# A planner told other TensorE times, and the end of the last norm spread over three engines

## The chip, the cores and the metric

The kernel runs on one core of one Trainium2 chip. The metric is device microseconds of one execution; a difference of about 0.2% is the least that a measurement of this kernel can tell from none. TensorE (PE; its weight loads are PEld) multiplies, VectorE (DVE) and ScalarE (ACT) do elementwise work, GpSimd (POOL) does small odd jobs, and SyncE (SP) issues every DMA.

## The reference, cut to what matters

Two decoder layers on 256 tokens of width 1024, all in float32. Layer 0 mixes tokens by a gated unit in chunks of 128, layer 1 by attention with 16 heads (256 tokens are one block, so it is plain causal attention with a relative bias). After each mixer comes a gated MLP of width 2816 with a causal convolution of width 3. Each of the four sub-layers ends in

```
x = layer_norm(alpha * x + f(x), g, b)      # over the 1024 columns of each token
y = (x - mean) * rsqrt(var + eps) * g + b
```

The last of these norms is the output. The kernel computes it for a tile of 128 tokens in two steps: first `(x - mean) * g`, then `that * rstd + b`.

## The kernel before, in words

Tokens lie in two tiles of 128 (`t` = 0, 1). A float32 product is made of three products of split operands (`hi*hi`, `hi*lo`, `lo*hi`, type float32r); for a weight chunk of 1 MB, ScalarE writes `whi` (a rounded copy) and VectorE `wlo` (the rest). One step (`rows_step`, line 553) for one row block `k`, one tile `t` and 512 output columns is a group of three matmuls.

Nothing is issued as it is written down. Every operation is recorded in a `Plan` (line 74) with an engine, an estimated time and its dependencies. `Plan.emit` (line 122) then runs a list scheduler over the records and issues everything in the order that this yields. TensorE's bulk groups keep their recorded order; short groups marked `fill` (transposes, attention, spatial mixing) go in as soon as the plan says that they are ready. On the other engines the operation that can start first is taken, and among those that can start together the one with the earliest due time; when these are equal, the one that became a candidate first. Between engines the plan adds `LATE` (line 82: pe 200, act 140, dve 130, pool 200 ns, and 150 more when TensorE is the one that waits, line 213), and 130 ns between dependent operations of one engine. For a DMA, SP is taken to be held for 475 ns. These engine queues are in order on the chip: an instruction that waits holds all that stand behind it on its engine, and all DMAs stand in SP's one queue.

The estimates: a float32r matmul of n columns `max(107, n/2.4) + 2.5` ns (line 322), a float32 one 218 ns up to 128 columns and `n/0.6 + 5` above, a transpose 110 ns; VectorE's `stt` (line 346) 130 + 1.04 n with a per-token scalar, 70 + 1.04 n without; `ts` (line 350) 187 + 0.52 n; an activation (line 335) 93 + 0.833 n, and 93 more for each per-token operand. `plan.later(ns, fn)` records `fn` once TensorE's recorded time has advanced by `ns`; `plan.tick(AHEAD)` records what falls due in the next 12 us.

`project_out` (line 583) is the last product of each sub-layer, with its norm. It runs all but the last 6 row blocks for both tiles, then finishes tile 0: its first 512 columns over the 6 blocks, then its other 512. Then tile 1: 512 columns, and two pieces of 256 columns in banks of their own. `stats` (line 487) adds each finished piece to the residual, runs bn_stats on it, aggregates, adds eps, and has GpSimd raise the variance to -0.5 (line 500) for `rstd`. For the inner norms `ln_back` (line 518) normalizes on VectorE (`ts`, line 351), turns the tile with transposes (fills, line 332) and splits it for the next product. For the last norm `scaled` (line 504) does the two steps on VectorE, in two halves of 512 columns and in four pieces of 256, each stored by a DMA of 128 KB (line 355). The end of tile 1's `scaled` is the end of the kernel.

Of the kernel before, what the change touches and what calls it, by code (L numbers as in the profile page):

```python
# [12 lines left out]
F32R = mybir.dt.float32r  # L13
AF = mybir.ActivationFunctionType
ALU = mybir.AluOpType
# [3 lines left out]
P = 128  # L19
D = 1024  # L20
# [5 lines left out]
NT = S // P  # L26
# [9 lines left out]
HALF = 512  # L36
# [11 lines left out]
AHEAD = 12000  # L48
# [167 lines left out]
def flat(ap):  # L216
    n = 1
    for d in ap.shape[1:]:
        n *= d
    return n  # L220
# [3 lines left out]
def trunk_kernel(ctx: ExitStack, tc: tile.TileContext, a: dict, out: bass.AP):  # L224
    nc = tc.nc
    plan = Plan()
# [58 lines left out]
    def bank(long=False):  # L285
        free = [i for i in ALONE if not bank_of[i][2]]
        return taken(min(free, key=lambda i: bank_of[i][0]), long) if free else half(long)
# [29 lines left out]
    def mms(seq, r, w, fill=False):  # L317

        ns = 0.0
        for o, l, x, _, _ in seq:  # L320
            n = flat(x)
            ns += max(107.0, n / 2.4) + 2.5 if l.dtype == F32R else (218.0 if n <= P else n / 0.6 + 5)

        def emit():
            for o, l, x, start, stop in seq:
                nc.tensor.matmul(o, l, x, start=start, stop=stop)  # L326
        plan.op("pe", ns, emit, r, w, fill)

    def transposes(seq, r, w):
        def emit():  # L330
            for o, x in seq:
                nc.tensor.transpose(o, x, ident.ap)  # L332
        plan.op("pe", 110.0 * len(seq), emit, list(r) + [ident], w, True)

    def act(o, x, func, r, w, bias=None, scale=None, accum=None, psum=False, table=None):
        kw = {k: v for k, v in (("bias", bias), ("scale", scale), ("accum_out", accum)) if v is not None}
        ns = (51 if psum else 93) + 0.833 * flat(x) + 93 * (sum(not isinstance(v, float) for v in kw.values()))
        plan.op("act", ns, lambda: nc.scalar.activation(o, x, func, **kw), r, w, table=table)  # L338

    def dve(ns, emit, r, w):  # L340
        plan.op("dve", ns, emit, r, w)
# [4 lines left out]
    def stt(o, x, s, y, op0, op1, r, w):  # L346
        dve((70 if isinstance(s, float) else 130) + 1.04 * flat(x),
            lambda: nc.vector.scalar_tensor_tensor(o, x, s, y, op0=op0, op1=op1), r, w)  # L348
# [4 lines left out]
    def load(o, src, w, r=(), nbytes=None, rank=None):  # L353
        nbytes = nbytes or flat(o) * P * 4
        plan.op("sp", nbytes / 360.0, lambda: nc.sync.dma_start(o, src), r, w, nbytes=nbytes, rank=rank)  # L355
# [50 lines left out]
    def sub(name, c, s):  # L406
        return chunks[where[name, c]][s]

    def spent(name, c):
        i = where[name, c] + CHUNKS  # L410
        if i < len(stream):
            prep(i)


    def const(name, cols):
        return Buf(sb.tile([P, cols], F32, name=name))

    ident, nhalf = const("ident", P), const("nhalf", 1)
# [4 lines left out]
    def xt_new():  # L423
        return xth.new(), xtl.new()
# [24 lines left out]
    def ln_rows(i):  # L449
        b = rowring.new()  # L450
        src = a["lnrow"]
        load(b.ap, bass.AP(tensor=src.tensor, offset=src.offset + i * 2 * D, ap=[[0, P], [1, 2 * D]]), [b])
        return b, b.ap.rearrange("p (a d) -> p a d", a=2)
# [47 lines left out]
                [(st, ["ve"]), nhalf], [(st, ["rstd"])])  # L501
        return st, mv[:, 0:1], rstd

    def scaled(r, x, st, mean, rstd, rows, to=None):

        rb, rv = rows
        for o in range(0, D, HALF):
            sl, parts = slice(o, o + HALF), range(o // S, (o + HALF) // S)
            stt(x[:, sl], x[:, sl], mean, rv[:, 0, sl], ALU.subtract, ALU.mult,
                [(r, parts), (st, ["mv"]), rb], [(r, parts)])  # L510
        for o, n in [(o, S) for o in range(0, D, S)]:
            sl, parts = slice(o, o + n), range(o // S, (o + n) // S)
            stt(x[:, sl], x[:, sl], rstd, rv[:, 1, sl], ALU.mult, ALU.add,
                [(r, parts), (st, ["rstd"]), rb], [(r, parts)])
            if to is not None:
                load(to[:, sl], x[:, sl], (), [(r, parts)])

# [65 lines left out]
    def project_out(name, nk, at, xold, li, rows_i):  # L583

        last = li is None

        rows = None if name == "b_o" else ln_rows(rows_i)


        pieces = [[(o, HALF, bank(True)) for o in (0, HALF)] for _ in range(NT)]  # L590
        cuts = [[(0, HALF), (HALF, HALF)], [(0, HALF), (HALF, S), (HALF + S, S)]]
        ends = []

        def step(t, k, which, first=0, last=nk - 1):
            hi, lo = sub(name, k // 2, k % 2)
            hk, lk, r = at(k, t)
            rows_step(which, hk, lk, r, hi, lo, k == first, k == last)

        start = nk - TAIL
        for k in range(start):  # L600
            for t in range(NT):
                step(t, k, pieces[t][:1])
                step(t, k, pieces[t][1:], last=nk - 1 if t == 0 else start - 1)
            if k % 2:
                spent(name, k // 2)
        res = (None, None) if last else xt_new()
        for t in range(NT):
            r, x = xold[t], xold[t].ap

            def add(o, n, b, by=ALPHA):  # L610
                parts = range(o // S, (o + n) // S)
                stt(x[:, o:o + n], x[:, o:o + n], by, b.ap[:, :n], ALU.mult, ALU.add, [(r, parts), b], [(r, parts)])
                done_with(b)

            mine = list(pieces[t])
            if t == NT - 1:
                add(*mine.pop())
                ends = [(o, n, half()) for o, n in cuts[t][1:]]
                mine += ends
            for p in mine:  # L620
                for k in range(start, nk):
                    if t == 0 and k == nk - 2:
                        plan.tick(AHEAD)
                    step(t, k, [p], first=start if p in ends else 0)
            if t == NT - 1:
                for k in range(start, nk, 2):
                    spent(name, k // 2)

            rows = rows or ln_rows(rows_i)
            st, mean, rstd = stats(r, x, cuts[t], lambda j, o, n: add(*mine[j], 1.0 if mine[j] in ends else ALPHA))  # L630
            if last:
                scaled(r, x, st, mean, rstd, rows, out[t * P:(t + 1) * P, :])
            else:
                ln_back(r, st, mean, rstd, rows, t, li, *res, T0_WAITS if t == 0 else T1_WAITS)
        return res
# [244 lines left out]

    at = gmlp()
    h, l = project_out("a_out", KT, at, xtok, 0, 1)
    at = conv_up(0, h, l)
    scr = build_bias(10 * S)
    h, l = project_out("f_dn0", FT, at, xtok, 1, 2)
    at = moba(h, l, scr)
    h, l = project_out("b_o", KT, at, xtok, 2, 3)
# [82 lines left out]
```

## Time and profile before

| | us |
|---|---|
| median of 3 runs | 572.33 (572.28 to 572.41) |
| profiled execution | 571.2 |
| its span, first to last instruction | 569.5 |

| engine | busy us | share of the span |
|---|---|---|
| PE | 556.1 | 98% |
| DVE | 464.3 | 82% |
| ACT | 359.2 | 63% |
| POOL | 11.5 | 2% |

The chain of work that ended last is 95% PE. A busy share is an average over stages: a gain counts only where that engine's work is what ends last. Busy PE means that matmuls are in flight, and the trace models their ends, so the distance between starts is what shows its pace.

### The profile page before, as it was taken

What the parts mean: (1) busy time and instruction counts of PE and PEld (TensorE: products, weight loads), DVE (VectorE), ACT (ScalarE), POOL (GpSimd) and SP (SyncE); (2) the same over time, 40 slices, a digit from 0 to 9 for tenths busy, and PEclk for the clock granted to TensorE, in tenths of its full rate; (3) what the DMA queues carried; (4) which work ended last, traced back from release to release, by engine and by line L of the source; (5) the groups of instructions that cost most, each with busy time, mean ns of one, the idle gap of its engine ahead of it and who ended that gap; (6) DMA issues with size and microseconds to landing.
All of it is one profiled execution on the core that took longest, in us unless ns stands there. A gap on an engine that the chain in (4) does not pass through costs nothing.

```text
span 569.5 us, 8289 instructions
## 1 busy us (share of the span) xinstructions
PE 556.1 (98%) x3098; PEld 474.9 (83%) x3098; DVE 464.3 (82%) x873; ACT 359.2 (63%) x652; POOL 11.5 (2%) x17
## 2 busy tenths in 40 slices
PE   6999999999999999999999999999999999999994
PEld 4799888888888878888888877788888888888884
DVE  5598989999999997467958988579989999996526
ACT  5555558776777686335578877377777767775300
POOL 0020010000000000001000000010000000000001
PEclk9999999999999999999999999999999999999998
DMA  7897435547554577742665653506455556566302
GB/s 266 330 361 283 181 146 182 189 153 279 171 211 155 216 229 266 270 165 74 222 221 185 194 210 115 222 2 221 156 218 219 201 174 218 195 242 229 147 1 74
DMA packets 20132, 110.92 MB, mean 195 GB/s; under 512 B 2251, under 2 KB 6268, under 8 KB 7676
## 3 DMA queue, kind: packets, MB, share of 16 engines
q1 hardware_dynamic: 20092, 110.39, 54.2%
q8 instruction: 24, 0.39, 0.3%
q14 instruction: 16, 0.13, 0.1%
HBM read 109.31 MB, written 1.07 MB: 194 GB/s over the span
## 4 chain that ended last, share of the span: by engine, by line
PE 95%; DMA 2%; DVE 1%; SPq 0%; ACT 0%; issue 0%; DVEq 0%
PE twos L326 52%; PE bank L326 41%; DMA raw<-in_a_v 2%; PE bank L332 1%; PE twos L332 1%; DVE wlo L344 0%; DVE x L348 0%; SPq L355 0%; ACT whi L338 0%; DVE stat L494 0%; DVEq L966 0%; DVE stat L497 0%; DVE stat L499 0%; DVE xt L344 0%
## 5 line engine op out<-in xcount | busy, mean ns | idle before, releaser
L344 DVE TENSOR_TENSOR wlo<-raw,whi 128x1024 fp32r<-128x1024 f32 (+1 forms) x212 | 228.2, 1099 | 33.7 <-ACT whi L338 32.8
L338 ACT ACTIVATE whi<-raw 128x1024 fp32r<-128x1024 f32 (+1 forms) x212 | 194.8, 954 | 55.1 <-DMA raw<-in_f_dn 21.3
L326 PE MATMUL twos<-xt,whi 128*128 128x512 f32 x640 | 222.2, 394 | 0.0
L326 PE MATMUL twos<-xt,wlo 128*128 128x256 f32 x640 | 177.3, 277 | 0.0
L326 PEld LDWEIGHTS twos<-xt,whi 128*128 128x128 f32 x640 | 120.0, 188 | 27.8
L326 PE MATMUL bank<-whi,rr 128*128 128x512 f32 x432 | 135.5, 391 | 0.0
L326 PEld LDWEIGHTS twos<-xt,wlo 128*128 128x128 f32 x640 | 120.1, 188 | 0.1
L326 PEld LDWEIGHTS bank<-whi,rr 128*128 128x128 f32 x432 | 81.1, 188 | 17.9 <-issue 1.0
L326 PE MATMUL bank<-wlo,rr 128*128 128x512 f32 x216 | 84.0, 389 | 0.0
L326 PE MATMUL bank<-xt,whi 128*128 128x256 f32 (+1 forms) x256 | 71.0, 348 | 0.0
L348 DVE SCALAR_TENSOR_TENSOR ff<-ff,convc 128x254 f32<-128x254 f32 (+1 forms) x160 | 69.6, 478 | 0.3
L338 ACT ACTIVATE ff<-twos 128x512 f32<-128x512 f32 (+1 forms) x56 | 30.8, 565 | 47.9 <-PE twos L326 44.8
L326 PE MATMUL bank<-xt,wlo 128*128 128x256 f32 x192 | 54.0, 281 | 0.0
L326 PEld LDWEIGHTS bank<-xt,whi 128*128 128x128 f32 x256 | 44.0, 190 | 6.8 <-issue 1.0
L326 PEld LDWEIGHTS bank<-wlo,rr 128*128 128x128 f32 x216 | 40.6, 188 | 8.0
L338 ACT ACTIVATE ff<-ff,convc 128x256 f32<-128x256 f32 x80 | 45.6, 592 | 1.9 <-DVE ff L344 1.2
L344 DVE TENSOR_TENSOR ff<-twos,ff 128x512 f32<-128x512 f32 (+1 forms) x48 | 30.9, 645 | 15.3 <-ACT ff L338 13.0
L326 PE MATMUL twos<-whi,xt 128*128 128x512 f32 x128 | 42.1, 396 | 0.0
L338 ACT ACTIVATE ff<-bank,lncol 128x128 f32<-128x128 f32 x48 | 18.8, 458 | 29.1 <-PE bank L332 29.1
L326 PEld LDWEIGHTS bank<-xt,wlo 128*128 128x128 f32 x192 | 36.4, 190 | 0.0
L348 DVE SCALAR_TENSOR_TENSOR x<-x,bank 128x512 f32<-128x512 f32 x16 | 11.0, 686 | 25.0 <-PE bank L326 25.0
L326 PEld LDWEIGHTS twos<-whi,xt 128*128 128x128 f32 x128 | 24.1, 188 | 4.8
(71 smaller groups left out, 489.1 us busy)
## 6 DMA issues: line engine op xcount, KB each, us to landing
raw<-in_f_up SPq DMA_DIRECT2D x44, 1024.0 KB, 4.8
raw<-in_f_dn SPq DMA_DIRECT2D x22, 1024.0 KB, 4.9
raw<-in_b_qk SPq DMA_DIRECT2D x8, 1024.0 KB, 4.9
lnrow<-in_lnrow SPq DMA_DIRECT2D x5, 1024.0 KB, 6.7
raw<-in_a_u SPq DMA_DIRECT2D x4, 1024.0 KB, 5.1
raw<-in_a_out SPq DMA_DIRECT2D x4, 1024.0 KB, 5.0
raw<-in_b_v SPq DMA_DIRECT2D x4, 1024.0 KB, 4.9
raw<-in_b_o SPq DMA_DIRECT2D x4, 1024.0 KB, 5.0
```

The source lines that it names most:

```text
L326: nc.tensor.matmul(o, l, x, start=start, stop=stop)
L332: nc.tensor.transpose(o, x, ident.ap)
L338: plan.op("act", ns, lambda: nc.scalar.activation(o, x, func, **kw), r, w, table=table)
L344: dve(70 + 1.04 * flat(x), lambda: nc.vector.tensor_tensor(o, x, y, op=op), r, w)
L348: lambda: nc.vector.scalar_tensor_tensor(o, x, s, y, op0=op0, op1=op1), r, w)
```

## The change

Three edits. First, the planner's estimates for TensorE: a float32r matmul becomes `n/2.4 + 13.4` ns, a float32 one `n/0.6 - 25`, a group whose stationary operand is under 128 in a dimension takes `0.68 * ns + 200`, and a group of transposes `60 + 93 * len`. No instruction changes by this, only the order in which the plan issues. Second, in `project_out` tile 0 finishes in another order: the last 6 row blocks run without the very last one for both halves, and then the last block for both. Third, in the very last norm (tile 1): the first step takes the upper 512 columns ahead of the lower, and the second step of columns 768 to 1023 goes to ScalarE (`* rstd`) and then GpSimd (`+ b`), with 600 ns as GpSimd's estimate; the other three pieces stay on VectorE.

```diff
@@ mms
-            ns += max(107.0, n / 2.4) + 2.5 if l.dtype == F32R else (218.0 if n <= P else n / 0.6 + 5)
+            ns += n / 2.4 + 13.4 if l.dtype == F32R else n / 0.6 - 25.0
+        if min(seq[0][1].shape) < P:
+            ns = 0.68 * ns + 200.0
@@ transposes
-        plan.op("pe", 110.0 * len(seq), emit, list(r) + [ident], w, True)
+        plan.op("pe", 60.0 + 93.0 * len(seq), emit, list(r) + [ident], w, True)
@@ scaled
-    def scaled(r, x, st, mean, rstd, rows, to=None):
+    def scaled(r, x, st, mean, rstd, rows, to=None, shared=False):
-        for o in range(0, D, HALF):
+        for o in (HALF, 0) if shared else (0, HALF):
...
-            stt(x[:, sl], x[:, sl], rstd, rv[:, 1, sl], ALU.mult, ALU.add,
-                [(r, parts), (st, ["rstd"]), rb], [(r, parts)])
+            if shared and o + n == D:
+                act(x[:, sl], x[:, sl], AF.Copy, [(r, parts), (st, ["rstd"])], [(r, parts)], scale=rstd)
+                plan.op("pool", 600, lambda sl=sl: nc.gpsimd.tensor_tensor(x[:, sl], x[:, sl], rv[:, 1, sl], op=ALU.add),
+                        [(r, parts), rb], [(r, parts)])
+            else:
+                stt(x[:, sl], x[:, sl], rstd, rv[:, 1, sl], ALU.mult, ALU.add,
+                    [(r, parts), (st, ["rstd"]), rb], [(r, parts)])
@@ project_out
-            for p in mine:
-                for k in range(start, nk):
-                    if t == 0 and k == nk - 2:
-                        plan.tick(AHEAD)
-                    step(t, k, [p], first=start if p in ends else 0)
+            todo = [(p, k) for p in mine for k in range(start, nk)]
+            if t == 0:
+                todo.sort(key=lambda x: x[1] == nk - 1)
+            for p, k in todo:
+                if t == 0 and k == nk - 2:
+                    plan.tick(AHEAD)
+                step(t, k, [p], first=start if p in ends else 0)
...
-                scaled(r, x, st, mean, rstd, rows, out[t * P:(t + 1) * P, :])
+                scaled(r, x, st, mean, rstd, rows, out[t * P:(t + 1) * P, :], t == NT - 1)
```

## Rows read from the trace of the kernel before

**Rows 1.** Busy time by stretch: us, each engine's busy us (instructions), PEclk, DMA share, GB/s.
```profile
0.00:20.40 20.40, 14.64 (x49) 10.99 (x50) 9.72 (x21) 10.28 (x17) 0.70 (x6) 1.00 0.83 295
20.40:561.90 541.50, 541.50 (x3049) 463.92 (x3049) 450.49 (x843) 348.87 (x635) 9.88 (x10) 1.00 0.54 193
561.90:569.50 7.60, 0.00 (x0) 0.00 (x0) 4.14 (x10) 0.00 (x0) 0.92 (x1) 0.63 0.21 69
```

**Rows 2.** Waits of PE: for whom, us in total, times, longest us.
```profile
PE bank L326 <- DVE xt L361: 4.9, 1, 4.9
PE bank L326 <- DVE wlo L344: 0.8, 1, 0.8
```

**Rows 3.** The chain that ended last, its head: start us, us, what.
```profile
10.08 0.69 DVE wlo L344
...
10.79 7.21 DMA raw<-in_a_v
...
19.12 1.24 DVE wlo L344
...
20.40 19.62 PE bank L326 x119
```

**Rows 4.** Timeline of PE: start us, us, engine, line, operation, out<-in, shape, count.
```profile
75.51 0.27 PE L332 MATMUL bank<-ident,x 128*128 128x128 f32 x1
...
530.00 0.62 PE L326 MATMUL bank<-whi,rr 128*128 128x512 f32 x2
...
530.68 0.62 PE L326 MATMUL bank<-whi,rr 128*128 128x512 f32 x2
```

**Rows 5.** Timeline of SP's queue at the end.
```profile
565.02 0.33 SPq L355 DMA_DIRECT2D out<-x  x1
...
565.42 0.41 SPq L355 DMA_DIRECT2D out<-x  x1
...
565.93 0.39 SPq L355 DMA_DIRECT2D out<-x  x1
...
566.42 0.40 SPq L355 DMA_DIRECT2D out<-x  x1
```

**Rows 6.** Timeline of DVE at the end (a count merges instructions).
```profile
563.20 0.74 DVE L348 SCALAR_TENSOR_TENSOR x<-x,stat,lnrow 128x512 f32<-128x512 f32 x1
...
563.86 1.14 DVE L348 SCALAR_TENSOR_TENSOR x<-x,stat,lnrow 128x512 f32<-128x512 f32 x2
...
564.52 0.87 DVE L348 SCALAR_TENSOR_TENSOR x<-x,stat,lnrow 128x256 f32<-128x256 f32 x2
...
565.31 0.87 DVE L348 SCALAR_TENSOR_TENSOR x<-x,stat,lnrow 128x256 f32<-128x256 f32 x2
```

**Rows 7.** Timeline of POOL.
```profile
1.08 0.29 POOL masks.py:199 TENSOR_SCALAR_AFFINE_SELECT ident<-ident 128x128 f32<-128x128 f32 x1
31.57 2.01 POOL L459 TENSOR_SCALAR_AFFINE_SELECT ff<-ff 128x1024 f32<-128x1024 f32 x1 [30.20 <-DMA ff<-in_wsT]
...
73.56 0.93 POOL L500 TENSOR_TENSOR stat<-stat,nhalf 128x1 f32<-128x1 f32 x1 [37.05 <-DVE stat L499]
...
259.29 0.55 POOL L500 TENSOR_TENSOR stat<-stat,nhalf 128x1 f32<-128x1 f32 x1 [176.03 <-DVE stat L499]
269.10 1.39 POOL L500 TENSOR_TENSOR stat<-stat,nhalf 128x1 f32<-128x1 f32 x1 [9.26 <-DVE stat L499]
370.86 0.55 POOL L500 TENSOR_TENSOR stat<-stat,nhalf 128x1 f32<-128x1 f32 x1 [100.36 <-DVE stat L499]
...
563.42 0.92 POOL L500 TENSOR_TENSOR stat<-stat,nhalf 128x1 f32<-128x1 f32 x1 [6.97 <-DVE stat L499]
```

**Rows 8.** Timeline of DVE beside POOL's operations at 31.57 and 269.10.
```profile
30.27 2.36 DVE L344 TENSOR_TENSOR wlo<-raw,whi 128x1024 fp32r<-128x1024 f32 x2 [0.53 <-ACT whi L338]
...
268.88 1.22 DVE L344 TENSOR_TENSOR wlo<-raw,whi 128x1024 fp32r<-128x1024 f32 x1
```

**Rows 9.** Groups by form, ACT: busy us, mean ns of one, idle before.
```profile
L338 ACT ACTIVATE ff<-ff,smax 128x256 f32<-128x256 f32 x16 | 8.0, 501 | 3.3 <-DVE smax L832 3.3
```

**Rows 10.** Timeline of DVE at the first inner norm, tile 0.
```profile
71.63 0.69 DVE L348 SCALAR_TENSOR_TENSOR x<-x,bank 128x512 f32<-128x512 f32 x1 [0.87 <-PE bank L326]
...
74.52 1.00 DVE L351 TENSOR_SCALAR x<-x,stat 128x512 f32<-128x512 f32 x2 [0.44 <-POOL stat L500]
```

## The prediction

> **What bounds the kernel now.** I read the busy time by stretch first. From 20.40 to 561.90 us PE is busy for 541.50 of 541.50 us; before that it is busy 14.64 of 20.40, and in the last 7.60 us not at all [rows 1]. So the span has three parts with three limits. A busy PE could still be slowed, so I looked at the distance between starts: three matmuls of 512 columns start every 530.68 - 530.00 = 0.68 us, 227 ns each, at the full granted clock (1.00, which is 2.4 GHz) [rows 1, 4]. The waits agree: PE itself waited only 4.9 and 0.8 us, both in the head [rows 2]. So the 541.5 us in the middle are instructions and not stalls; the change removes none of these, hence a new order cannot shorten them and can only put stalls in. In the head the chain hangs on a weight chunk that was issued at 10.79 and took 7.21 us to land; PE went on at 20.40 [rows 3]. In the end part the chain is VectorE, then SP's four DMA issues and the landing [rows 5, 6].
>
> **Part 1, the planner's times.** For 512 columns the estimate goes from 512/2.4 + 2.5 = 215.8 ns to 226.7, and the rows show 227 [rows 4]: the plan's PE was 5% too fast and is now right. In the middle that is worth nothing, for the reason above. In the head: the issue at 10.79 follows the VectorE instruction at 10.08, which ended at 10.77 and freed the buffer [rows 3]; the landing and the split behind it are no choice of the plan. I cost the head at 0, with -0.8 (PE's whole stall, rows 2) to +0.3 (my estimate: half of a 0.69 us VectorE instruction that slips ahead) as bounds.
>
> What a new order could cost is a fill that stands too early in PE's queue: it holds the bulk behind it until its data is there. This must be taken with part 2.
>
> **Part 2, tile 0's last block at the end.** Before, VectorE's add of the first half was hidden under the 6 groups of the second. Now the halves end one group (0.68 us) apart, so the add and the bn_stats of the first half move onto tile 0's chain. VectorE has two adds and two bn_stats from about 0.65 us before the end of the last group; an add's 0.69 us [rows 10] for each, less what overlaps, makes the statistics some 0.6 us later (estimate: one more 0.69 us instruction less the 0.08 us by which neighbours overlap; 564.52 + 0.87 - 2 x 0.395 shows such an overlap, rows 6).
>
> Does a fill notice? The transposes of this tile came at 75.51 [rows 4], and their first input was ready at about 74.52 + 0.55 = 75.07 [rows 10], so they had 0.44 us to spare. In the plan of before, the chain from the last group to the transposes adds up to 200 + 602 + 130 + 602 + 130 + 90 + 130 + 70 + 130 + 465 + 200 + 453 + 280 = 3482 ns, which is 5.4 groups of 647: they go in after 6. That fits the trace, 6 x 0.68 = 4.08 us before 75.51 being 71.43, where the first group of tile 1 belongs. In the new plan both adds and both bn_stats count: 200 + 3 x 602 for what stands ahead of the aggregate, and so on, some 3954 ns, 5.8 groups of 680: again 6. So the plan gives no more room, while the chip needs 0.6 more than 0.44: a stall of about 0.2 us at this norm. There GpSimd's power took 0.93 us; at the two other inner norms it took 0.55 [rows 7], which leaves 0.2 us to spare. I take +0.2 for the three; bounds 0 and 3 x 0.65 = 1.95 (each power as long as the longest, 1.39 [rows 7]: 0.2 + 0.46). In the last norm the shift of tile 0 disappears: its work is done long before PE ends at 561.90, and VectorE idles before that.
>
> **Part 3, the end.** One of four VectorE pieces goes, 0.395 us apiece by its starts (565.31 - 564.52 is two) [rows 6]. But that is not what ends last: the four DMA issues start at 565.02, 565.42, 565.93 and 566.42, and while the first two gaps follow the data, SP spends about 0.5 us on each [rows 5]. The fourth piece was done at 565.31 + 0.87 = 566.18 and its DMA started 0.24 us later. So a quicker VectorE saves at most 0.05 us here (four issues at 0.45); what counts is when each of the four DMAs can go, and in which order they stand.
>
> The new piece: the power ends at 563.42 + 0.92 = 564.34 [rows 7]; ScalarE starts some 0.03 us later (74.52 against 73.56 + 0.93, rows 7, 10) and needs 501 ns, the mean of one of 256 columns with a per-token operand [rows 9], so GpSimd is asked at 564.9. The trace has no such add. What GpSimd's rows show is that it waits for VectorE: the power takes 0.55 us when VectorE is idle, but 1.39 when it started 0.22 us into a `wlo` that ran until 270.10; it ended 0.39 after that [rows 7, 8]. The select of 1024 columns ended 0.96 us after VectorE's `wlo` at 32.63 [rows 7, 8]. So the add starts where a VectorE piece ends, at 564.99 or 565.39, and then takes between 0.41 us (0.29 for 128 columns [rows 7] and 128 more at 0.96/1024 us each) and 0.89 (0.41 and 256 columns twice, for two inputs, at that rate). That is an end between 565.40 and 566.28; I take the middle, 565.84.
>
> Of the rules on this, the Trainium skill's page GPSIMD Engine Reference (section 3.1 Elementwise) gives 4497 ns for an add of 2048 columns; an estimate from it is 0.56 us for 256, which no row here shows; the sum would move by less than 0.1.
>
> Now the order. In the plan, VectorE does the upper half first, then the lower. When both are done, piece 512 is ready at once (the upper half is long finished), pieces 0 and 256 only 130 ns later, so VectorE runs 512, 0, 256. Counting from the end of the aggregate (ns): 512 runs from 1524 to 1920, 0 to 2316, 256 to 2712; ScalarE starts at 995, GpSimd ends at 995 + 399 + 140 + 600 = 2134. The DMAs are ready at 2050 (512), 2334 (768), 2446 (0), 2842 (256); SP takes 512 at 2050, is free at 2525, and there finds 768 and 0, equally due, 768 a candidate first. So I expect SP's order 512, 768, 0, 256, with GpSimd's piece second, and two finished pieces queued behind it. On the chip: 512 at 565.02; 768 at 565.84 + 0.05; 0 at 566.39; 256 at 566.88, against 566.42 before: +0.45 us. Bounds: +0.04 (an end at 565.40) to +0.89 (566.28).
>
> **Sum.** Against the profiled execution (span 569.5, time 571.2): head 0, middle +0.2, end +0.45, that is 571.85. That execution is 1.1 us below the median of the runs, so I put the difference on the median: 572.33 + 0.65 = 573.0 us.
>
> **Rivals.**
> *Stalls at the inner norms (slower).* Place: the first transposes of tile 0. If VectorE runs a `wlo` of 1024 columns just when the power starts, the power takes 1.39 and the stall is 0.65. Two of three norms and the end's 0.45 give 572.33 + 0.2 + 1.3 + 0.45 = 574.3; it decides from one such norm beside the 0.2 and 0.45 on. For: the plan keeps 6 groups, and VectorE has such splits at hand. Against: in the rows of tile 0 this happened at no inner norm.
>
> *GpSimd waits for all three pieces (slower).* VectorE's pieces start before the last one ends, so GpSimd may find no gap until 565.39 + 0.395 = 565.79. Then it ends at 565.79 + 0.65 = 566.44, and two DMAs follow it: 566.49 + 2 x 0.49 = 567.47, +1.05, with the 0.2 in all 573.6. Against: the power that was asked at 563.42 came in behind the piece that ended at 563.94 and was done 0.40 later, although VectorE had started its next at 563.86 [rows 6, 7]. The Trainium skill (SBUF — State Buffer, section Who interferes with whom) would have it this way: the two share one port pair as an exclusive lock for a whole instruction, and whoever issues first has it. The row on one column speaks against a wait beyond one piece; no row has a GpSimd operation of 256 columns with two inputs there.
>
> *The end costs nothing (same).* SP keeps 768 last, or the add is at its lower bound, and the fills fit: 572.4.
>
> *The head gets shorter (faster).* PE idles 20.40 - 14.64 = 5.8 us there [rows 1]. The stall before 20.40 alone is 0.8 and would stay within what counts as no change; if PE also began 0.5 us earlier, the time would be 572.33 - 1.3 = 571.0 with nothing lost behind it. Against: the chunk's issue hangs on a buffer, not on an estimate [rows 3], and the first loads stand in a fixed order of their own.
>
> **Chances.** Forecast 0.47, end costs nothing 0.13, stalls 0.22, GpSimd behind all three 0.11, head 0.07. No change within 0.2% (1.14 us, about what can be told here): 0.60; slower 0.33; faster 0.07. The forecast alone ranges from 572.4 to 573.5. The range for all: up to 574.5, which takes in two long stalls, and down to 571.9, since little is left below no change.
>
> **What would show it.** PE's busy share stays whole from its 20.4 us on, with waits under `L332` of a few tenths at most; the add of the first half and the second stand side by side at 71 us; SP's second issue at the end waits for GpSimd, and the last starts near 566.9 if PE ends at 561.9. The GpSimd add ends within a piece's time of a VectorE end. Wrong, if PE's last matmul ends more than 0.5 us earlier or 1 us later, or if 768 is issued last.

## The result, and the profile after

The changed kernel takes 577.25 us (median of 6 runs, 574.74 to 580.14), the kernel before 572.31 beside it (570.97 to 573.08): ratio 1.0094 [1.0075, 1.0112]. Forecast were 573.0 us, 571.9 to 574.5. The profiled execution took 576.77 us, its span 575.1 (575.05 to the hundredth).

The windows first, PE's busy time and the granted clock (columns as in [rows 1]). The second fence is the kernel before over the third stretch.

```profile
20.40:38.00 17.60, 17.16 (x103) 15.06 (x102) 13.56 (x21) 12.04 (x15) 2.80 (x3) 1.00 0.92 335
38.00:62.00 24.00, 21.57 (x164) 20.89 (x163) 20.17 (x36) 12.84 (x20) 0.00 (x0) 0.93 0.67 250
62.00:567.10 505.10, 505.06 (x2784) 428.95 (x2782) 415.38 (x790) 328.07 (x600) 5.79 (x7) 1.00 0.52 183
567.10:575.10 8.00, 0.00 (x0) 0.00 (x0) 4.21 (x9) 0.51 (x1) 1.93 (x2) 0.67 0.20 66
```
```profile
38.00:62.00 24.00, 24.00 (x188) 23.28 (x188) 21.79 (x39) 13.97 (x23) 0.00 (x0) 1.00 0.73 267
```

The middle is no longer whole: PE idles 0.44 and 2.43 us in two stretches where it never idled before. PE's last matmul starts at 566.78 instead of 561.62, 5.16 us later; from there to the span's end it is 8.28 us against 7.88, 0.40 more. PE's waits name the place (us in total, times, longest):

```profile
PE bank L328 <- DVE xt L363: 5.0, 1, 5.0
PE twos L328 <- DVE ff L346: 2.2, 1, 2.2
PE bank L328 <- DVE wlo L346: 0.9, 2, 0.4
PE twos L328 <- DVE ff L350: 0.2, 1, 0.2
```

The first and third are waits for first weights, as in [rows 2] (before it was one of 0.8 that ended at 20.40; now it is two of 0.44, and one of them falls at 22.86 us). The second is new. In PE's timeline it stands in layer 0's gated unit, at the spatial mixing (`twos<-ff`, a fill among the a_u matmuls), and the clock falls behind it:

```profile
53.62 0.28 PE L328 MATMUL bank<-xt,wlo 128*128 128x256 f32 x1
...
53.98 0.28 PE L328 MATMUL bank<-xt,wlo 128*128 128x256 f32 x1
56.48 0.71 PE L328 MATMUL twos<-ff 128*128 128x128 f32 x4 [2.23 <-DVE ff L346]
...
58.10 0.41 PE L328 MATMUL bank<-xt,wlo 128*128 128x256 f32 x1
...
58.74 0.41 PE L328 MATMUL bank<-xt,wlo 128*128 128x256 f32 x1
```
```profile
57.75:61.10 3.35, 3.35 (x19) 3.35 (x18) 3.35 (x7) 2.88 (x6) 0.00 (x0) 0.51 1.00 416
```

Three matmuls of 256 columns take 53.98 - 53.62 = 0.36 us before the wait and 58.74 - 58.10 = 0.64 after it: for 3.35 us the granted clock is 0.51, the lower of its two levels. PE stays busy all that time, so no wait shows these 3.35 x 0.49 = 1.64 us.

How much the gated unit lost in all is read from the same two matmuls in both traces, the first of a_u and the first of the projection behind it (after, then before):

```profile
30.93 0.40 PE L328 MATMUL bank<-xt,whi 128*128 128x256 f32 x2
...
62.48 0.40 PE L328 MATMUL bank<-whi,rr 128*128 128x512 f32 x1
```
```profile
31.23 0.40 PE L326 MATMUL bank<-xt,whi 128*128 128x256 f32 x2
...
57.80 0.40 PE L326 MATMUL bank<-whi,rr 128*128 128x512 f32 x1
```

The first starts 0.30 us earlier than before and the second 4.68 later: 4.98 us are lost between them. Idle 2.43 and clock 1.64 make 4.07 of these; the other 0.9 were not taken apart (the fills stand in six groups there instead of five). Behind the gated unit another 0.48 us come in steps of some tenths, and the end adds its 0.40.

The chain of waits in the changed kernel shows how it got there (start, us, what):

```profile
32.36 1.41 DVE wlo L346
33.79 7.25 DMA raw<-in_a_u
41.12 1.07 ACT whi L340
42.21 2.37 DVE wlo L346 x2
44.60 7.68 DMA raw<-in_a_out
52.31 1.07 ACT whi L340
53.40 2.36 DVE wlo L346 x2
```

A raw buffer is freed by the `wlo` of its chunk and then takes the next chunk: each late landing makes the next issue late. SP's queue shows who got in between (after):

```profile
29.00 0.33 SPq L357 DMA_DIRECT2D raw<-in_a_u  x1
29.37 0.72 SPq L357 DMA_DIRECT2D x<-in_x  x1
33.79 0.33 SPq L357 DMA_DIRECT2D raw<-in_a_u  x1
```

A load of x, 512 KB that VectorE first reads near 71 us [rows 10], now stands ahead of the last a_u chunk. Before, it stood behind both:

```profile
29.77 3.22 SPq L355 DMA_DIRECT2D raw<-in_a_u  x2
33.04 0.42 SPq L355 DMA_DIRECT2D x<-in_x  x1
```

ScalarE's splits in order, after and then before:

```profile
41.12 2.01 ACT L340 ACTIVATE whi<-raw 128x1024 fp32r<-128x1024 f32 x2 [3.52 <-DMA raw<-in_a_u]
...
52.31 2.01 ACT L340 ACTIVATE whi<-raw 128x1024 fp32r<-128x1024 f32 x2 [2.95 <-DMA raw<-in_a_out]
```
```profile
37.82 2.01 ACT L338 ACTIVATE whi<-raw 128x1024 fp32r<-128x1024 f32 x2 [0.26 <-DMA raw<-in_a_u]
...
47.93 2.00 ACT L338 ACTIVATE whi<-raw 128x1024 fp32r<-128x1024 f32 x2
```

The last a_u chunk is split 3.3 us later and the second a_out chunk 4.4 us later (52.31 against 47.93). ScalarE and VectorE work in order, so behind the second split stood the mixing's additions, on VectorE until 53.40 + 2.36 = 55.76; the one that freed PE's bank ran at 56.01, and PE went on at 56.48.

The end in its timelines:

```profile
568.58 0.92 POOL L502 TENSOR_TENSOR stat<-stat,nhalf 128x1 f32<-128x1 f32 x1 [6.49 <-DVE stat L501]
570.12 1.01 POOL L517 TENSOR_TENSOR x<-x,lnrow 128x256 f32<-128x256 f32 x1 [0.62 <-ACT x L340]
```
```profile
569.67 0.88 DVE L350 SCALAR_TENSOR_TENSOR x<-x,stat,lnrow 128x256 f32<-128x256 f32 x2
570.46 0.95 DVE L350 SCALAR_TENSOR_TENSOR x<-x,stat,lnrow 128x256 f32<-128x256 f32 x1
```
```profile
570.18 0.33 SPq L357 DMA_DIRECT2D out<-x  x1
571.15 0.33 SPq L357 DMA_DIRECT2D out<-x  x1
571.59 0.38 SPq L357 DMA_DIRECT2D out<-x  x1
572.06 0.40 SPq L357 DMA_DIRECT2D out<-x  x1
```

SP's second issue stands at 571.15, right behind GpSimd's end at 571.13; the two behind it follow at SP's own pace of 0.44 to 0.47 us, and the last stands 572.06 - 566.78 = 5.28 us behind PE's last matmul, against 4.80 before [rows 5]. VectorE's last piece takes 0.95 instead of 0.48 beside GpSimd's add.

### The profile page after: what moved, and what is told of

Same layout as the page of the kernel before. It is cut to its first block, busy times and chain, and to the rows that moved or that the text cites. A ratio compares the mean times of both kernels' runs of the same rounds, so it can differ in the third digit from the quotient of the medians.

```text
span 575.1 us, 8258 instructions
## 1 busy us (share of the span) xinstructions
PE 558.7 (97%) x3098; PEld 476.4 (83%) x3098; DVE 464.1 (81%) x872; ACT 363.9 (63%) x653; POOL 11.2 (2%) x18
## 4 chain that ended last, share of the span: by engine, by line
PE 89%; DMA 6%; DVE 3%; ACT 1%; SPq 1%; issue 0%; DVEq 0%; ACTq 0%
PE twos L328 51%; PE bank L328 36%; DMA raw<-in_a_v 2%; DMA raw<-in_a_u 2%; DVE wlo L346 2%; DMA raw<-in_a_out 1%; PE bank L334 1%; PE twos L334 1%; ACT whi L340 1%; SPq L357 1%; DVE x L350 0%; DVE stat L496 0%; DVE ff L346 0%; DVEq L976 0%; DVE stat L499 0%
## 5 line engine op out<-in xcount | busy, mean ns | idle before, releaser
L328 PE MATMUL bank<-xt,whi 128*128 128x256 f32 (+1 forms) x256 | 72.6, 354 | 0.0
L350 DVE SCALAR_TENSOR_TENSOR ff<-ff,convc 128x255 f32<-128x255 f32 (+1 forms) x160 | 69.5, 479 | 0.5 <-ACT ff L340 0.4
L328 PEld LDWEIGHTS bank<-xt,whi 128*128 128x128 f32 x256 | 45.2, 195 | 7.0 <-issue 1.0
L340 ACT ACTIVATE rr<-ff 128x256 fp32r<-128x256 f32 x52 | 20.9, 406 | 13.2 <-DVE ff L346 13.0
```

## The experiments

Medians are over 4 to 10 runs of a kernel, ratios against the kernel before on the same chip (its medians were 570.9 to 571.5 for e1 to e18, and 572.3 for the changed kernel). "At 31" and "at 61" are how much later than in the profile of before the same matmul starts: the first of a_u, and one of the projection that starts at 61.0 us there. What stands at 31 comes from the head, which differs by up to 1.5 us even where nothing in it was changed (e10, e12); the difference of the two is what the gated unit lost. "f_up" is the number of matmuls that PE has in flight in 100 to 200 us and in 395 to 495 us, in the f_up stages (the long product with the f_up weights) of the two convolution units. "End" is from the last matmul's start to the span's end. The last four columns are from one profile of each kernel.

```
kernel                              us      ratio [95%]              at 31  at 61   f_up      end
before                              -       -                         -      -      579 579   7.88
after                               577.25  1.0094 [1.0075, 1.0112]  -0.3   +4.7    579 579   8.28
e1_costs_only                       574.89  1.0061 [1.0043, 1.0079]  +0.1   +2.8    567 579   7.88
e2_sort_only                        571.38  1.0006 [0.9990, 1.0022]  -0.1   -0.1    579 579   7.87
e3_tail_only                        570.91  0.9994 [0.9981, 1.0007]  -0.4   -0.4    579 579   8.28
e4_without_f32r_cost                573.26  1.0048 [1.0027, 1.0070]  -0.1   -0.1    579 568   8.28
e5_x_after_a_u                      574.38  1.0056 [1.0034, 1.0079]  -1.2   -0.9    569 579   8.28
e6_x_early_in_before                571.25  0.9996 [0.9976, 1.0016]  +0.1   +0.1    578 578   7.88
e7_f32r_estimate_only               576.14  1.0089 [1.0059, 1.0119]  +0.6   +2.1    567 580   7.87
e8_landing_2500                     576.65  1.0088 [1.0056, 1.0120]  -0.8   -0.8    568 580   8.27
e9_split_behind_mixing              576.18  1.0088 [1.0060, 1.0116]  -1.0   +1.1    568 580   8.27
e10_tail_add_on_vectore             571.25  0.9991 [0.9971, 1.0011]  -1.5   -1.5    579 579   7.74
e11_f32r_estimate_from_conv         576.13  1.0083 [1.0057, 1.0110]  -1.3   -1.3    568 579   8.27
e12_x_behind_a_out                  571.30  0.9998 [0.9978, 1.0018]  +1.2   +1.2    579 579   7.88
e13_transposes_later                575.61  1.0068 [1.0042, 1.0095]  +0.2   +0.4    568 568   8.27
e14_transposes_earlier_in_before    571.74  0.9999 [0.9978, 1.0020]  -0.3   +0.2    579 579   7.88
e15_repaired_without_shared_end     574.90  1.0066 [1.0035, 1.0097]  -0.5   -0.5    569 568   7.88
e16_transposes_after_two_pairs      573.63  1.0056 [1.0036, 1.0077]  -0.2   -0.1    579 579   7.88
e17_transposes_after_six_pairs      575.75  1.0069 [1.0047, 1.0091]  -0.4   -0.2    569 570   7.88
e18_change_with_early_transposes    574.82  1.0070 [1.0046, 1.0094]  -0.8   +3.8    579 578   8.28
```

### Which part of the change costs (e1 to e4, e7)

e1 is the kernel before with part 1, e2 with part 2, e3 with part 3 of the diff; e4 is the changed kernel with one of the four estimates as before, e7 the kernel before with that one new:
```
-            ns += n / 2.4 + 13.4 if l.dtype == F32R else ...              (e4; e7 the other way round)
+            ns += max(107.0, n / 2.4) + 2.5 if l.dtype == F32R else ...
```

> Only the four new TensorE estimates. The trace after shows all of the loss of TensorE's end (561.91 to 567.07 us) arising between 38 and 61 us, in layer 0's gated unit, with a wait of 2.2 us of a spatial fill for VectorE and a half-clock stretch behind it. Theory A (the new estimates reorder SP and VectorE there): about 576.8 us, +4.5 on before, the same wait near 54 us, no loss at the end. Theory B (tile 0's new finishing order does it): 572.3 +- 0.5. Theory C (the end and the norms, as predicted): 572.3.

> Only tile 0's last row block moved to the end. Theory A: 572.3 to 572.8, no wait of TensorE near 54 us, at most 0.2 us under the transposes of the inner norms. Theory B: about 576.8 with the wait near 54 us.

> Only the last norm's piece on ScalarE and GpSimd. Theories A and B: TensorE ends as before (561.9 of the span), the stretch from there to the end grows from 7.59 to about 8.03 us as in the trace after: 572.75 us. If the end costs nothing by itself: 572.3. GpSimd's add about 1.0 us, VectorE's last piece near 0.95 instead of 0.48, SP's second issue waiting for GpSimd.

> The whole change but for the estimate of the float32r matmuls, which stays n/2.4 + 2.5. SP's order of the x loads is then that of before. Theory A with the float32r term as its cause: 572.7 to 573.2 (the end's 0.45 and small stalls), no wait near 54 us. If the other estimates or the finishing order do it: 576 to 577.

> The kernel before with one of the four new estimates: a float32r matmul n/2.4 + 13.4 ns instead of max(107, n/2.4) + 2.5. Of the four this alone moves a load of x ahead of the last chunk of a_u. Theory L: most of the loss of all four together (ratio 1.0061), so 573.5 to 575.5 us with a wait for ff of 1 us or more near 51 to 57 us. Rival V (it takes all four estimates together, which move 460 rows of VectorE's queue against 404 here): 571 to 573 us and no such wait.

The planner's times alone (e1) are slower, if less than expected; the order of the pieces (e2) and the shared end (e3) alone can't be told from before. Without the float32r estimate (e4) the wait near 54 us is gone. With that estimate alone (e7) the kernel is as slow as with the whole change within the intervals, and x stands ahead of the last a_u chunk too; but the gated unit loses 1.5 us and not 5, and the wait for `ff`, which was expected, did not come. PE's one wait there is for ScalarE:

```profile
61.86 0.49 PE L326 MATMUL bank<-whi,rr 128*128 128x512 f32 x1 [0.46 <-ACT ff L338]
```

The second a_out chunk is split at 52.26 us in e7, as late as in the changed kernel, but PE's last fills went in at 51.34: none stood there to wait. So the wait takes the float32r estimate (e4) and the other estimates besides (e7; e1 with all four has 1.2 us of it).

e4 is slower than before all the same: its end is 0.40 longer, and its second f_up stage loses some 2 us to something that no wait shows (568 matmuls against 579).

### Is it the load of x, or the order behind it? (e5, e6, e8, e9, e12)

e5 puts the loads of x behind the last a_u chunk again, by one more dependency in the plan; e6 puts one ahead of it in the kernel before (in SP's queue both then stand ahead), e12 both behind a_out; e9 leaves x early and has the second a_out chunk split behind the mixing; e8 has the planner expect late landings.
```
 e5  -load(xtok[t].ap, a["x"][:, t, :], [(xtok[t], QUART)])
     +load(xtok[t].ap, a["x"][:, t, :], [(xtok[t], QUART)], [(raw_of["a_u", 3], range(8))])
 e9  +if g == 5:                       # in spatial(g), late = split of a_out's second chunk
     +    for o in late: o.deps.add(plan.ops[-1])
 e8  -bus = max(bus, s + 1100.0) + o.nbytes / 360.0
     +bus = max(bus, s + 2500.0) + o.nbytes / 360.0
```

> The changed kernel with one more condition in the plan: both loads of x come behind the last chunk of a_u in SyncE's queue, as the kernel before has them; all else, the estimates too, is as in the changed kernel (8 of SyncE's rows, 29 of VectorE's and 14 of ScalarE's stand elsewhere). Theory L (the 512 KB of x that went ahead of the last a_u chunk delay that chunk, and everything behind it): the wait of TensorE for ff at the spatial mixing (2.2 us, then half clock for 3.4 us) goes, the bulk matmuls from 61 us on stand within 1 us of the kernel before instead of 4.6 later, 572.0 to 573.0 us with the end's 0.4. Rival V (the order on VectorE and ScalarE, splitting a late chunk ahead of the spatial mixing's small operations, does it whatever SyncE's order): the wait stays at 1 to 2.2 us and the time at 575 to 577.5.

> The kernel before with one more condition in the plan: one load of x stands between the last two chunks of a_u in SyncE's queue, as the change has it; estimates, order of the pieces and the last norm are as before. Theory L: the last a_u chunk lands later, the spatial mixing waits 1 to 3 us for ff, 574 to 577 us. Rival V: under the old estimates the spatial mixing's operations keep their place ahead of the late chunk's split, no wait over 0.5 us, 571 to 573 us.

> The changed kernel with the planner's estimate for the start of a transfer 2500 ns instead of 1100 ns, so that chunks land later in its plan and are split later in VectorE's and ScalarE's queues; SyncE's queue then has both last chunks of a_u ahead of bs, x behind two chunks of a_out. Theories L and V both: the split of a chunk that has not landed no longer stands ahead of the spatial mixing's operations, the wait for ff near 54 us goes; 571.5 to 573.5 us. If late landings as such (the transfers of 7 to 8 us a chunk) starve the stage whatever the order: 575 us or more, with TensorE waiting for whi or wlo there instead of ff.

> The changed kernel with one more condition in the plan: the split of the second a_out chunk (whi on ScalarE, wlo on VectorE) comes behind the first addition of the spatial mixing's group 5; the loads of x stay ahead of the last a_u chunk, as the change has them. Theory LV (the chunk lands 4 to 5 us later than before, and only because its split stands ahead of the mixing's small operations on engines that work in order does TensorE wait): no wait of TensorE for ff over 0.5 us near 54 us, bulk matmuls 1 us or less later than the kernel before at 61 us, 572.0 to 575.0 us by the pace of the stage after it. Rival L (what is late is the weights themselves, the order does not matter): the wait only moves to wlo or whi of that chunk, still 3 us or more behind at 61 us, 576 to 578 us.

> The kernel before, with both loads of x behind the four chunks of a_out in SyncE's queue (x is first needed at the projection's end, near 70 us); nothing else. Theory L taken further: each 512 KB taken out from among the chunks of the gated unit lets these land 1 to 1.5 us earlier; the kernel gains what TensorE still waits for chunks there, 0.5 to 1.5 us: 569.5 to 571 us against 571.3. If TensorE waits for nothing there any more (the profile of the kernel before has no wait from 24 to 75 us): no change, 571 to 571.6 us. If x then lands too late for the projection's addition: a wait for x near 70 us and 572 us or more.

With x behind (e5) the stretch is mended but for 0.3 us: there is no wait for `ff`, and the matmuls at 61 us start 0.9 us earlier than before (1.2 at 31 us). Yet x early does no harm to the kernel before (e6): there the plan put the late chunk's split behind the mixing. ScalarE's row in e6 still waits for a landing, but with the mixing's work done ahead of it:

```profile
52.25 0.71 ACT L338 ACTIVATE rr<-ff 128x256 fp32r<-128x256 f32 x2
53.58 2.01 ACT L338 ACTIVATE whi<-raw 128x1024 fp32r<-128x1024 f32 x2 [0.61 <-DMA raw<-in_a_out]
```

e9, which changes only that position, keeps two waits (longest us last) in place of the one of 2.2, and the clock stays at 1.00; the gated unit still loses 2.0 of the 5.0 us:

```profile
PE twos L327 <- DVE ff L349: 0.7, 1, 0.7
PE twos L327 <- DVE ff L345: 0.6, 1, 0.6
```

So the position accounts for three fifths of the loss; the rest stays open. Ahead of the first of the two waits stands the `wlo` of the first a_out chunk (47.20 + 2.36 = 49.56 us), which e9 leaves where the change put it, so the same cause is likely there, but no run moved that chunk. e6 shows that a late chunk by itself costs PE nothing, e7 that even an early split costs little when no fill of PE stands behind it: the wait needs the late landing, the split queued in front of small work, and a fill that needs this work at that moment.

e8 mends the stretch too (0.0 between 31 and 61 us), and e12 gains nothing, as the rival expected. But the totals of e5, e8 and e9 stayed 3 to 5 us above before: my expectations from the wait alone (571.5 to 573.5 us over e5 and e8, 572 to 575 for e9) were wrong. In all three the first f_up stage runs at 568 or 569 matmuls per 100 us, some 2 us. In e8 that is the smaller part: it loses another 1.8 us around the norm at 275 us and 1.5 at the one at 388, with new waits of PE there (1.0 and 1.1 us).

### The end (e3, e10)

```
-plan.op("pool", 600, lambda sl=sl: nc.gpsimd.tensor_tensor(x[:, sl], x[:, sl], rv[:, 1, sl], op=ALU.add), ...)
+tt(x[:, sl], x[:, sl], rv[:, 1, sl], ALU.add, [(r, parts), rb], [(r, parts)])
```

> The kernel before with the change's last norm, but the addition of the last 256 columns on VectorE instead of GpSimd (ScalarE still multiplies them by rstd). If GpSimd's addition is what the end pays for (it waits for a VectorE piece, and VectorE's next piece for it): span minus TensorE's end 7.59 us as in the kernel before, within 0.1, against 8.03 in the changed kernel; total 570.5 to 572 us. If the other order of the first step or ScalarE's part in it costs the 0.44: 7.9 us or more.

"End" is 8.27 to 8.28 in each of the nine kernels with GpSimd's add and 7.87 to 7.88 in ten of the eleven without. In the eleventh, e10, which keeps ScalarE's part and the new order but has the add on VectorE, it is 7.74: GpSimd's add is what the end pays for. In the totals these 0.4 us are too small to tell (e3 is 0.9994).

### The second pace in the f_up stages (e11, e13 to e18)

There each weight tile is a pair of matmuls, 512 columns and 256. From the starts in the traces the fast stream repeats two pairs in 693 ns (231, 112, 233, 117), the slow one three pairs in 1060 (232, 118, 241, 120, 236, 113): 0.451 and 0.460 ns a column, 2.1 us a stage, at a granted clock of 1.00 with PE busy throughout. Two stretches, first of e13 and then of e14:

```profile
100.00:200.00 100.00, 100.00 (x568) 86.67 (x567) 94.84 (x166) 77.10 (x127) 0.00 (x0) 1.00 0.55 200
395.00:495.00 100.00, 100.00 (x568) 86.77 (x567) 93.85 (x163) 77.06 (x127) 0.00 (x0) 1.00 0.55 200
```
```profile
100.00:200.00 100.00, 100.00 (x579) 87.45 (x578) 93.55 (x161) 71.97 (x122) 0.00 (x0) 1.00 0.54 195
395.00:495.00 100.00, 100.00 (x579) 87.44 (x578) 93.07 (x160) 74.78 (x125) 0.00 (x0) 1.00 0.54 195
```

In the seven stages that run four pairs or more ahead of the four transposes, the stream has the slow rhythm from its start (pairs start 350, 361, 349 ns apart). Which one holds for the stage is settled where these transposes interrupt it, a few pairs in: the fast one, where it comes, starts right behind them. The first suspect was the copy by ScalarE that the transposes wait for. In the kernel before ScalarE idles ahead of it; in e5 it does one more `whi` first, and the copy comes some 35 ns too late. The rows are e5's and before's:

```profile
90.96 1.66 ACT L340 ACTIVATE whi<-raw 128x512 fp32r<-128x512 f32 x3
92.52 0.56 ACT L759 COPY ff<-twos 128x512 f32<-128x512 f32 x1
```
```profile
93.23 0.59 ACT L749 COPY ff<-twos 128x512 f32<-128x512 f32 x1 [2.22 <-PE twos L326]
93.72 1.67 ACT L338 ACTIVATE whi<-raw 128x512 fp32r<-128x512 f32 x3
```

A late copy is not needed for the slow pace, though: in e4, e7 and e8 ScalarE idles ahead of it as well and the copy ends 264 to 269 ns ahead of the first transpose, as in before (264), and yet the stage is slow. e4's row:

```profile
390.79 0.59 ACT L759 COPY ff<-twos 128x512 f32<-128x512 f32 x1 [0.26 <-PE twos L328]
```

e11 gives the new float32r estimate only from the first convolution unit on (`new_f32r = True` at the head of `conv_up`). e13 to e18 change only the planner's duration of that copy (e13, e15 600; e14 100; e16, e18 200; e17 1300), which moves the transposes by a pair or more: e14 in the kernel before, e18 in the changed kernel, the others in e5, of which e15 to e17 have the end of before:
```
-plan.op("act", 480, lambda y=y, b=b: nc.scalar.copy(y.ap, b.ap), [b], [y])
+plan.op("act", 600, lambda y=y, b=b: nc.scalar.copy(y.ap, b.ap), [b], [y])
```

> The changed kernel with the new float32r estimate only from the first convolution unit on; the gated unit and its projection are planned with the old one (SyncE's order there has both a_u chunks ahead of x). Theory LV: no wait for ff near 54 us, bulk matmuls within 0.5 us of the kernel before at 61 us; what is left is the end's 0.44 and, if the slower pace of the f_up0 stage (0.460 instead of 0.451 ns a column, 2.1 us) goes with the new estimate in that stage, 2.1 us: 573.5 to 574.5 us. If the pace is set by how the stage is entered and not by the new order inside it: 571.4 to 572.5 us. Rival: the loss is spread over all stages and only shows at 54 us: 575 us or more.

> The changed kernel with both loads of x behind the last a_u chunk, and the planner's duration of ScalarE's copy ahead of the convolution unit's four transposes 600 instead of 480 ns, which puts these transposes one pair of matmuls later in TensorE's queue in both convolution units. Theory R (the transposes' wait of 3 to 60 ns for the copy throws the matmul stream behind them into the slower of two rhythms): no wait, 0.451 ns a column in f_up0 and f_up1, 571.6 to 572.6 us, 2 us or more below the same kernel without this edit (574.38), and a narrower spread. Rival P (the pace belongs to the new order as such, or to chance): 0.460 in f_up0 again, 573.5 to 575 us.

> The kernel before with the planner's duration of the same copy 100 instead of 480 ns: the four transposes stand one pair of matmuls earlier in TensorE's queue in both convolution units and must wait some 0.1 to 0.3 us for the copy. Theory R: 0.460 ns a column in one or both f_up stages (of eight profiled stages with a wait there six had it), 573 to 576 us, spread of 3 us or more. Rival P: 0.451 in both, only the waits themselves, 571.2 to 572.2 us.

> The first kernel of this call with the last norm as before (all of its second step on VectorE): the change's new estimates and its order of the pieces, x behind a_u, the transposes later. If nothing but the three named places costs: 570.8 to 571.8 us, the kernel before within 0.2%. If the new estimates are worth something elsewhere (fewer small waits at the norms): below 570.5 us. If a fourth cost is left: 572.3 us or more.

> The new estimates and the new order of the pieces, x behind a_u, the last norm as before, and the planner's duration of ScalarE's copy 200 instead of 480 ns: the four transposes stand after two pairs of matmuls in both convolution units (after three in the kernel before and the changed kernel, after four where it was 600). Theory Q (the place in the stream's three-pair cycle decides the rhythm): 0.451 ns a column in f_up0 and f_up1, 570.8 to 572 us, the kernel before within 0.2%. Rival N (the new order makes the rhythm slow wherever the transposes stand): 0.460 in one or both, 573.5 us or more.

> As the kernel with two pairs, with a planned copy of 1300 ns: the transposes stand after six pairs of matmuls, where nothing of theirs is late. Theory Q, taken by the cycle of three pairs: 0.451 in both stages as after three, 570.8 to 572.3 us. If the place decides but not by threes, or under rival N: 0.460 in one or both, 573.5 us or more.

> The changed kernel, x loads and shared end included, with the planned copy 200 instead of 480 ns alone: transposes after two pairs. Theory Q: fast rhythm in both stages, and what is left is the wait at 54 us (2.6 to 4.6 us) and the end's 0.44: 574 to 576.3 us, 1 to 3 us below the changed kernel's 577.25. Rival N: no change, 576.5 to 578 us, with 0.460 in one stage or both.

e11 keeps the gated unit whole and has the slow pace in its first stage, so it does not come from there; at 576.13 us it also missed its 573.5 to 574.5. Nor does it take the new float32r estimate: e4 has the old one and a slow second stage. All 14 stages under the old estimates are fast, and of those under any of the new ones 13 in 26 are slow. Theory R fell: in e13 nothing waits at the transposes (they start 108 ns apart, as in before) and both stages are slow; in e14 they wait and both are fast:

```profile
93.76 0.28 PE L326 MATMUL twos<-xt,wlo 128*128 128x256 f32 x1
94.03 0.66 PE L332 MATMUL bank<-ident,ff 128*128 128x128 f32 x4
```

(0.27 us from the last matmul of 256 columns to the first transpose, instead of 0.12.) Over all 20 profiles (40 stages; the wait is what the first two starts of the transposes come later, counted from the matmul ahead of them, than in the kernel before): after three pairs 14 of 14 without a wait are fast; after four or six pairs, with no wait over 4 ns, 6 of 6 are slow (one stage after five, with a wait of 5 ns, is fast). So without a wait the place counts. After three pairs with a wait of 2 to 70 ns 7 of 9 are slow, with one of 85 to 210 ns 4 of 4 are fast. After two pairs 6 of 6 are fast, but all of these wait 200 ns or more, so that their place and their long wait are not told apart. My rule by threes fell with e17. Why TensorE falls into one rhythm or the other was not found.

e16 has no wait at 54 us, the fast pace twice and the old end, and is still 1.0056 [1.0036, 1.0077], against an expected 570.8 to 572 us: a fourth cost. In its profile the same matmuls start 0.1 us earlier than before at 61 us, then later by 0.3 us at 97 and 207, 0.6 at 273, 1.1 at 311 and 1.6 at 393 us: steps of some tenths at the transposes, the norms and in the attention, no wait over 0.23 among them. They were not taken apart. (e15 was to show such a cost, but with the slow pace in both stages it can't.)

e18 came within its expected time, and has the fast pace in both stages. So has the changed kernel in its profile, however. Against the kernel before beside each, e18 is 3.9 us slower and the changed kernel 4.9, and the intervals of the two ratios overlap: how much of the change's median the pace makes up, in runs that were not profiled, is not shown. What e18's profile keeps is the wait at 54 us (1.9 us, then the lower clock again, 4.5 us in the gated unit), the end (8.28) and the small steps.

No kernel tried beats the one before; e2, e3, e6, e10, e12 and e14 equal it.

## Why the prediction was wrong

**The failed step** is in the bound: "a new order cannot shorten them and can only put stalls in", and after it, of part 1, "In the middle that is worth nothing, for the reason above". I then looked for stalls at the transposes of tile 0 alone and sized the middle at +0.2 (0 to 1.95 at three norms). The new times move work on all engines, SP's loads too. What the runs showed in its place: 4.98 us lost in layer 0's gated unit, of which PE's idle time is 2.43 and the lower clock behind it 1.64. The new times put x ahead of the last a_u chunk (putting it back takes all but 0.3 us away, e5), the next chunks land late, and the split of one stands in front of the mixing (moving it takes 3.0 us away, e9). The float32r estimate is needed for it (e4) but does not bring the wait by itself (e7). What the other 2.0 us of e9 are is open.

The rows of before could have warned: in 38 to 62 us VectorE is busy 21.79 of 24.00 us, the last a_u chunk lands just before its split (ScalarE idles 0.26 us for it), and the raw buffers chain one landing to the next. A planner that is right where it was 5% too fast gives a new schedule, and its cost had to be bounded by the stretch with the least slack, not by the place of the other edit. The prediction's own sign of being wrong came: PE's last matmul stands 5.16 us later, where it allowed 1.

**"PE busy" as a bound.** I checked the spacing of 512-column matmuls [rows 4] and held a busy PE for a fixed time. It is not: the same stage at the same clock takes 2.1 us more or less by its rhythm. In the profiled run of the change this cost nothing, since both stages are fast there; its other runs, between 574.7 and 580.1 us, were not profiled.

**Part 2** was right in that it costs nothing that can be told: e2 is within the measurement. But its 0.2 us did not come, and for reasons that the working did not have. In e2 the plan put the transposes three matmuls of 256 columns later, not after 6 groups again; in the changed kernel they stand after 6, but GpSimd's power took 0.55 us there (78.70) instead of 0.93, and PE waited for nothing.

**Part 3** was right: +0.45 forecast for the last issue, +0.48 measured there and +0.40 at the span's end. The order 512, 768, 0, 256 and SP's second issue behind GpSimd came as worked out. GpSimd's add was asked at 569.53 + 0.51 = 570.04, its row begins at 570.12, inside VectorE's second piece, and takes 1.01 us against the 0.41 to 0.89 that were forecast. Read as the prediction read the power's rows, with a wait inside, it ended 571.13 - 570.55 = 0.58 us behind that piece (569.67 + 0.88), within the forecast; the rows can't tell this from an add that ran all the 1.01 us. VectorE's last piece took 0.95 beside it, hidden behind SP. The Trainium skill's page SBUF — State Buffer (section Who interferes with whom) says that the two share a port pair under an exclusive lock; that VectorE's last piece doubled beside the add agrees with it. The rival that GpSimd waits for all three pieces did not come: its add ended before VectorE's last piece (571.41). In the working, the select ended 33.58 - 32.63 = 0.95 us after VectorE's `wlo` and not 0.96, which moves nothing.

**The rivals.** Stalls were the right kind, at the wrong place: not at the inner norms, and 574.3 us was too little. The head gave nothing: at 20 us the changed kernel's matmuls start 1.0 us earlier, from 25 to 38 us 0.3 earlier, which is within what the head differs by itself.

## What to carry over

A planner whose durations are made truer gives another order everywhere, also of the DMA issues: bound it from the stretch where engines in order have the least slack, not from where the edit seems to act. A late transfer can be harmless until its consumer stands in an in-order queue ahead of work that the bottleneck needs. And count instructions per time in a long stage before and after: a loss at full busy share and full clock shows in no list of waits.

## What was not expected of the hardware

- Two lasting rhythms of the same matmul stream at a granted clock of 1.00: 579 or 568 matmuls in 100 us, held for a whole stage and settled where four transposes interrupt it. Three pairs in, a wait of 2 to 70 ns there went with the slow one in 7 of 9 stages, none or one of 85 ns and more with the fast one in 18 of 18.
- The clock at 0.51 for 3.35 us after one wait of 2.2 us: 1.64 us on top of it. After e1's wait of 1.2 us it stayed at 1.00.
- GpSimd's add of 256 columns took 1.01 us in its row, a wait perhaps included, and VectorE's piece beside it 0.95 instead of 0.48.
